# A hybrid encoder block: the gates of three token blocks as one stream of batches, the choice of experts by four ranks at a time, weights split a block ahead, and a wider output projection

## The chip, the core and the metric

The kernel runs on one core of a Trainium2 chip. The metric is the device time of one execution in microseconds (us); the time of a version is the median of its runs. The engines of the core are named as the profile names them: PE is TensorE (its matmuls), PEld its weight loads, DVE is VectorE, ACT is ScalarE, POOL is GpSimd, SP is SyncE, which issues most of the loads. Each engine works off its own queue in order, and an instruction that waits holds up what stands behind it in that queue.

## What is computed

One layer on 512 tokens of width 1024, in float32: `h = x + Mixer(RMSNorm(x))`, `h = h + PEER(RMSNorm(h))`, then a last RMSNorm. The mixer is one wide input projection, a gated recurrence (HGRN2), a long convolution by Fourier transforms (Hyena), two gated branch projections and an output projection `w_out`. PEER is a lookup of experts. For 8 heads a query is compared with two sets of 128 keys; the best 16 of each side give 256 sums, and the best 16 of these name 16 of 16384 experts:

```python
s1, i1 = lax.top_k(s[:, :, 0], PEER_TOPK)
s2, i2 = lax.top_k(s[:, :, 1], PEER_TOPK)
cand_s = (s1[..., :, None] + s2[..., None, :])          # 16 x 16 sums
top_s, pos = lax.top_k(cand_s, PEER_TOPK)
experts = jnp.take_along_axis(cand_i, pos, axis=-1)
g = jax.nn.softmax(top_s, axis=-1)
act = jax.nn.gelu(jnp.einsum('td,thkd->thk', xb, u)) * g   # u, v: rows of two tables
return jnp.einsum('thk,thkd->td', act, v)
```

## The kernel before

Tokens come in four blocks of 128. A float32 product is made of three matmuls on values split into a high part and a residual: `split` (lines 90 to 94) rounds on ACT (L93) and subtracts on DVE (L94), and `mm3` (lines 97 to 105) issues high by high and low by high in turn (L102, L103), then high by low (L105). A weight block of 1024 x 128 is loaded by SP, split into `whi` and `wlo` (two buffers each) and multiplied: 24 matmuls of 512 columns.

The mixer comes first. Its last part, `projected`, multiplies the merged branches by `w_out`. The split weights of `w_out` lie in four pairs of tiles of 256 columns (`load_wo`), so that each token block takes 4 times 24 matmuls of 256 columns (L1176), and each group of 24 is added to `h` by DVE (L1177).

`queries` then computes the scores of the 16 half heads (`hp`), each from one block of the weights `w_q`: a product (`proj`), a copy `qT` and a score product, and five DVE instructions per token block that find the best 16 (`top16`).

The experts are used in two ways. Token block 0 (`GTB`) fetches the rows of its chosen experts from memory with indirect loads by POOL. Token blocks 1, 2 and 3 (`DTB`, the dense blocks) are multiplied with all 16384 experts: a row `r` of 128 experts is 24 matmuls of 384 columns into `ps_a` (two buffers) and a gelu on ACT (`act_row`); later `combine` multiplies the gated result with the rows of the second table, 18 matmuls of 512 columns a row. For this the gates of the chosen experts have to be spread out into a matrix of 128 x 128 experts for each token.

That spreading is the part around the change:

- `select` picks, for four heads of one token block, the 16 best of 50 candidate sums and their expert numbers. It compares the positions with a list (`one`, L1288, bfloat16), multiplies with the candidate numbers (`exp`, L1290) and adds up (L1281). It works on two heads and eight ranks at a time; ranks 0 to 7 need only 20 of the 50 candidates. Four steps, two of 20 candidates (320 elements) and two of 50 (800 elements), make one call, and each token block takes two calls, one for each half of the heads (`part` 0 and 1). `one` is written with the rank innermost and read by L1290 with the candidate innermost, so that its neighbours in the reading lie 8 bfloat16 apart.
- `gates_out` takes one dense block. DVE splits each expert number into two indices `i1`, `i2` (L1313 to L1317), PE turns these and the gates (three transposes, L1323), ACT copies them out as `tr` and `tg` (L1324, L1325). Then come 32 batches of four tokens: DVE compares (`one`, L1334) and multiplies (`own`, L1337), ACT copies (`rows`, L1336), PE multiplies `own` by `rows` (L1344), four batches behind the preparation (`LAG`), and ACT copies the product to `Gs` (L1349), which SP writes to memory after eight batches. After its 32 batches a block runs its last five steps with no new batch, and then the next block's turning begins.
- `main` in `peer` strings this together: the last `select` of the first dense block, then for each block its `gates_out` with one step of the next block's `select` (for the last block: of the top 16 of token block 0) after every third step (`mixed`, `MIX`). `weave` puts one `act_row` in for each unit of a hand-set cost. `select` of token block 0 and the first steps of `combine` follow.

The order of the instructions on each engine is not the order of the code: a scheduler makes it from the dependencies, its own estimate of each duration, and the order of the code as priority. The order on each engine is then fixed.

Of the kernel before, what the change touches and what calls it, by code (L numbers as in the profile page):

```python
# [21 lines left out]
P = 128  # L22
L = 512
D = 1024
# [119 lines left out]
def proj(C, src, xh, xl, eng=None):  # L144

    hi, lo = load_w(C, src, eng=eng)
# [63 lines left out]
def mixer(C):  # L210
# [40 lines left out]

    def gates_b():
# [25 lines left out]
    with tc.tile_pool(name="yah", bufs=1, side="right") as yp:  # L278
# [11 lines left out]
        C.wos = []  # L290
# [12 lines left out]

def load_wo(C, pool, c):

    nc = C.nc
    if c % 2 == 0:
        C.wos.append((pool.tile([P, KB, 2 * P], F32R, name=f"woh{c}"), pool.tile([P, KB, 2 * P], F32R, name=f"wol{c}")))
    hi, lo = C.wos[c // 2]
    o = (c % 2) * P  # L310
# [11 lines left out]
def hyena(C, ctx, xh, xl, raws, fill):  # L322
# [112 lines left out]
    for half in range(D // HC):  # L435
# [94 lines left out]
        for fb in range(4):  # L530
# [16 lines left out]
            split(nc, Yi[0][:, fb], Yi[1][:, fb], t3)  # L547
        next(fill)
# [299 lines left out]
MIX = 3  # L848
# [3 lines left out]
LAG = 4  # L852
GQ = 32
# [16 lines left out]
def peer(C, ctx, mh, ml):  # L870
# [9 lines left out]
    pio = cp.tile([P, NPAIR, TOPK // 2], BF16, name="pio")  # L880
    with tc.tile_pool(name="pid", bufs=1) as ip:
        pid = ip.tile([P, NPAIR], F32, name="pid")
        nc.scalar.dma_start(pid, a["pair"].to_broadcast([P, NPAIR]))
        nc.vector.tensor_copy(pio, pid[:, :, None].to_broadcast([P, NPAIR, TOPK // 2]))
# [65 lines left out]
    with tc.tile_pool(name="gb", bufs=1) as gb, tc.tile_pool(name="slw", bufs=2) as sw, \  # L950
# [209 lines left out]
def projected(C, mh, ml, xh, xl, xg):  # L1160

    nc, tc, a = C.nc, C.tc, C.a
    with tc.tile_pool(name="wo4", bufs=1) as w4, tc.tile_pool(name="wo2", bufs=2) as wo2:
# [6 lines left out]
        for tb in range(TB):  # L1170
# [18 lines left out]
def queries(C, xh, xl, v16, i16, s0, chosen, fill):  # L1189
# [3 lines left out]
    with tc.tile_pool(name="slc", bufs=1) as cp, tc.tile_pool(name="slw0", bufs=2) as w2, tc.tile_pool(name="slw1", bufs=2) as sw:  # L1193
# [48 lines left out]
def select(C, w2, tb, part, v16, i16, gate, eid, pio, ahead=2):  # L1242
# [40 lines left out]
    H2, K2 = 2, TOPK // 2  # L1283
    for hd in range(0, H, H2):
        for k0, n in ((0, NFIRST), (K2, NPAIR)):
# [190 lines left out]
```

## Time and profile before

| | us |
|---|---|
| runs shown | 2046.88, 2050.67, 2050.99; median 2050.67 |
| profiled execution | 2054.18 |
| its span | 2052.4 |
| PE busy in it | 2020.1 (98%) |
| DVE busy in it | 1681.6 (82%) |
| ACT busy in it | 991.3 (48%) |
| POOL busy in it | 545.2 (27%) |

The span is the time from the first to the last instruction of the program on the core; 1.8 us of the profiled execution lie outside it. Places in the profile are given in us from the start of the span. The output projection runs from 723 to 771, `queries` to about 940, the gates of the dense blocks to 1163, and the last stage, rows and `combine` beside the fetched rows of token block 0, to the end. In rows of the timeline the columns are start, length, engine, line, operation and tiles, and in brackets the idle time of that engine just before, with what ended it. A matmul's length is longer than its distance to the next one, since matmuls overlap.

### The profile page before, as it was taken

Reading aid. Unit: us, or ns where it says so; the run is one execution under the profiler, and the core shown is the slowest. Engines: PE = TensorE matmul, PEld = TensorE weight load, DVE = VectorE, ACT = ScalarE, POOL = GpSimd, SP = SyncE. Lnnn points to the kernel's source line nnn. Section 1 sums busy time; section 2 is a strip of 40 time slices with the busy share of each in tenths; the row PEclk is TensorE's granted clock in tenths of the full one; section 3 lists DMA queues with packets and bytes.
Section 4 is the critical chain, followed back from the end, with each engine's and each line's share of the span. In section 5 each row is a group of like instructions: output and inputs, shape, how many; then the busy total and the mean of one; then the engine's idle time right before and its main releaser. Section 6 shows DMA issues by size and latency. Waiting matters only on the chain.

```text
span 2052.4 us, 30757 instructions
## 1 busy us (share of the span) xinstructions
PE 2020.1 (98%) x11625; PEld 1787.2 (87%) x11625; DVE 1681.6 (82%) x3036; ACT 991.3 (48%) x1473; POOL 545.2 (27%) x331
## 2 busy tenths in 40 slices
PE   8999999999999999999999999999999999999998
PEld 6888888888888898899999998888888888888887
DVE  6788853989986647979999877886887789889895
ACT  5555434777775623436776643333323323333333
POOL 0000000000000000000000017766766777766760
PEclk9999999999999999999999999999999999999999
DMA  5212213212122434224767788988998898999884
GB/s 193 84 52 68 72 52 112 72 63 79 66 73 73 152 127 144 98 72 159 223 189 241 234 305 335 338 317 316 347 345 302 322 367 334 350 345 343 317 295 171
DMA packets 160402, 417.96 MB, mean 204 GB/s; under 512 B 12890, under 2 KB 66012, under 8 KB 160126
## 3 DMA queue, kind: packets, MB, share of 16 engines
q1 hardware_dynamic: 115180, 263.58, 37.4%
q0 software_dynamic: 36864, 134.23, 17.8%
q10 hardware_dynamic: 8210, 18.19, 2.5%
q8 instruction: 91, 1.49, 0.3%
q14 instruction: 57, 0.47, 0.1%
HBM read 377.94 MB, written 38.01 MB: 203 GB/s over the span
## 4 chain that ended last, share of the span: by engine, by line
PE 85%; DVE 7%; DMA 3%; issue 3%; ACT 1%; POOL 0%; DVEq 0%; ACTq 0%; SPq 0%; POOLq 0%
PE ps_mm L102 10%; PE ps_mm L105 10%; PE ps_mm L103 10%; PE acc L1072 7%; PE acc L1073 7%; PE acc L1071 7%; PE ps_a L103 7%; PE ps_a L102 7%; PE ps_a L105 7%; PE ps_g L1344 3%; PE ps_x L666 1%; DMA grow<-in_u,gidx 1%; PE ps_x L102 1%; PE ps_x L105 1%; PE ps_x L103 1%
## 5 line engine op out<-in xcount | busy, mean ns | idle before, releaser
L102 PE MATMUL ps_a<-pxh,uh 128*128 128x384 f32 x1024 | 347.6, 339 | 4.6 <-ACT gact L931 4.5
L103 PE MATMUL ps_a<-pxl,uh 128*128 128x384 f32 x1024 | 345.0, 337 | 0.0
L94 POOL TENSOR_TENSOR ul<-uraw,uh 128x1024 fp32r<-128x1024 f32 x70 | 184.8, 2640 | 595.6 <-PE ps_a L105 446.2
L93 ACT CAST vh<-vraw 128x1024 fp32r<-128x1024 f32 x128 | 134.5, 1051 | 351.1 <-DMA vraw<-in_v 246.9
L1072 PE MATMUL acc<-vl,gh 128*128 128x512 f32 x768 | 300.6, 391 | 3.0 <-DVE vl L94 3.0
L1073 PE MATMUL acc<-vh,gl 128*128 128x512 f32 x768 | 300.2, 391 | 0.0
L1071 PE MATMUL acc<-vh,gh 128*128 128x512 f32 x768 | 298.8, 389 | 0.0
L102 PE MATMUL ps_mm<-xh,whi 128*128 128x512 f32 (+1 forms) x656 | 256.5, 393 | 0.4 <-ACT gt L255 0.4
L103 PE MATMUL ps_mm<-xl,whi 128*128 128x512 f32 (+1 forms) x656 | 252.2, 386 | 0.0
L1014 DVE SCALAR_TENSOR_TENSOR grow<-grow,xg 128x1024 f32<-128x1024 f32 x128 | 191.3, 1516 | 52.9 <-DMA grow<-in_u,gidx 52.8
L1026 DVE SCALAR_TENSOR_TENSOR xg<-grow,gw,xg 128x1024 f32<-128x1024 f32 x127 | 196.5, 1547 | 29.9 <-DMA grow<-in_v,gidx 28.3
L902 POOL IOTA iota<- 128x512 bf16 x1 | 1.2, 1189 | 770.8 <-PE ps_mm L105 770.8
L985 POOL DMA_INDIRECT grow<-in_u,gidx x128 | 188.7, 1474 | 51.1 <-issue 22.1
L102 PEld LDWEIGHTS ps_a<-pxh,uh 128*128 128x128 f32 x1024 | 193.2, 189 | 8.9 <-ACT gact L931 5.9
L105 PE MATMUL ps_a<-pxh,ul 128*128 128x384 f32 x1024 | 198.2, 334 | 0.0
L103 PEld LDWEIGHTS ps_a<-pxl,uh 128*128 128x128 f32 x1024 | 193.1, 189 | 3.0
L94 DVE TENSOR_TENSOR vl<-vraw,vh 128x1024 fp32r<-128x1024 f32 x128 | 180.4, 1410 | 3.4 <-ACT vh L93 3.4
L94 DVE TENSOR_TENSOR wlo<-wraw,whi 128x1024 fp32r<-128x1024 f32 x112 | 136.6, 1220 | 54.9 <-PE ps_mm L105 29.2
L985 POOL DMA_INDIRECT grow<-in_v,gidx x128 | 170.3, 1330 | 36.9 <-issue 20.2
L105 PEld LDWEIGHTS ps_a<-pxh,ul 128*128 128x128 f32 x1024 | 179.3, 188 | 0.1
L93 ACT CAST whi<-wraw 128x1024 fp32r<-128x1024 f32 x112 | 117.4, 1049 | 120.8 <-PE ps_mm L103 110.8
L93 ACT CAST uh<-uraw 128x1024 fp32r<-128x1024 f32 x128 | 134.5, 1051 | 84.9 <-PE ps_a L103 63.9
(417 smaller groups left out, 4079.7 us busy)
## 6 DMA issues: line engine op xcount, KB each, us to landing
uraw<-in_uT SPq DMA_DIRECT2D x128, 512.0 KB, 6.1
vraw<-in_v SPq DMA_DIRECT2D x128, 512.0 KB, 6.0
wraw<-in_w_in SPq DMA_DIRECT2D x80, 512.0 KB, 3.5
Gd<-Gs SPq DMA_DIRECT2D x12, 2048.0 KB, 9.7
gt<-Gd SPq DMA_DIRECT2D x32, 768.0 KB, 7.4
kept<-gact ACTq DMA_DIRECT2D x22, 384.0 KB, 3.5
gkept<-kept SPq DMA_DIRECT2D x22, 384.0 KB, 5.8
wraw<-in_w_q SPq DMA_DIRECT2D x16, 512.0 KB, 4.4
```

The lines of the kernel that those rows point to most:

```text
L93: nc.scalar.copy(hi, src)
L94: return (eng or nc.vector).tensor_sub(lo, src, hi).ins
L102: nc.tensor.matmul(out, ah, bh, start=(i == 0), stop=False)
L103: nc.tensor.matmul(out, *((al, bh) if late else (ah, bl)), start=False, stop=False)
L105: nc.tensor.matmul(out, *((ah, bl) if late else (al, bh)), start=False, stop=(stop and i == n - 1))
L985: nc.gpsimd.indirect_dma_start(out=t, out_offset=None, in_=tab, in_offset=bass.IndirectOffsetOnAxis(ap=gidx[:, j : j + 1], axis=0))
L1014: nc.vector.scalar_tensor_tensor(t, t, 1.0, xg, op0=ALU.mult, op1=ALU.mult, accum_out=gdot[h][:, i : i + 1])
L1026: nc.vector.scalar_tensor_tensor(gacc, t, gw[h][:, i : i + 1], gacc, op0=ALU.mult, op1=ALU.add)
L1071: nc.tensor.matmul(acc[k][c], gh[:, ts_], vh[:, ds_], start=(r == 0), stop=False)
L1072: nc.tensor.matmul(acc[k][c], gh[:, ts_], vl[:, ds_], start=False, stop=False)
L1073: nc.tensor.matmul(acc[k][c], gl[:, ts_], vh[:, ds_], start=False, stop=(r == NK - 1))
L1344: nc.tensor.matmul(pg[:, q * P : q * P + P], own[:, q], rows[:, q], start=True, stop=True)
```

## The change

Five edits.

1. `w_out`: the first four column blocks now share one pair of tiles of 512 columns, the others stay at 256 (`WIDE`). A token block takes 24 matmuls of 512 and 48 of 256 columns, and one addition of 512 and two of 256 columns.
2. Weights ahead: `queries` calls `load_w` (load, round, subtract) for the next block of `w_q` ahead of the product of the present one. `gates_b` does the same for the last four of its eight blocks (`C.early`).
3. `select` works on four heads and four ranks at a time (`RANKS`): again two steps of 320 and two of 800 elements a call, with the neighbours read by the multiplication now 4 bfloat16 apart.
4. `gates_out` is split. `gates_in` holds the indices, the transposes and the copies; it is issued at the end of the next block's `select`, while batches of the present block still run.
5. `gates_out` is now one stream of 96 batches over the three blocks, with no run-out between them, and `MIX` is 3, 2, 3 for the three blocks.

```diff
+def product(C, w, xh, xl):
+    hi, lo = w
...
     def gates_b():
+        w = None
         for db in range(KB):
-            ps = proj(C, a["w_in"][72 + db], xh, xl)
-            nc.scalar.activation(gts[db], ps, AF.Sigmoid)
+            now = w or load_w(C, a["w_in"][72 + db])
+            w = load_w(C, a["w_in"][73 + db]) if C.early and db < KB - 1 else None
+            nc.scalar.activation(gts[db], product(C, now, xh, xl), AF.Sigmoid)
...
+WIDE = {0: 4 * P, 4: 2 * P, 6: 2 * P}
...
-MIX = 3
+MIX = (3, 2, 3)
+RANKS = 4
...
+        ready = []
+        def chosen_and_turned(k):
+            yield from weighed(DTB[k], [part for part in range(2) if part or k >= EARLY])
+            ready.append(gates_in(C, gb, ps_g, DTB[k], gate, eid))
+            yield BATCH
         def main():
-            rest = [weighed(tb, [part for part in range(2) if part or k >= EARLY]) for k, tb in enumerate(DTB)]
-            yield from rest[0]
-            for k, tb in enumerate(DTB):
-                nxt = rest[k + 1] if k + 1 < len(DTB) else best(sw)
-                yield from mixed(gates_out(C, gb, go, ps_g, k, tb, gate, eid, iota), nxt, MIX)
+            yield from chosen_and_turned(0)
+            batches = gates_out(C, gb, go, ps_g, ready, iota)
+            for k in range(len(DTB)):
+                nxt = chosen_and_turned(k + 1) if k + 1 < len(DTB) else best(sw)
+                yield from mixed(islice(batches, P // 4), nxt, MIX[k])
+            yield from batches
...
-            for c, (hi, lo) in enumerate(C.wos):
+            for c, (hi, lo) in C.wos.items():
+                w = WIDE[c]
                 ps = C.ps_mm.tile([P, L], F32, name="ps_mm")
-                mm3(nc, ps[:, :256], [((mh[:, k, ts_], ml[:, k, ts_]), (hi[:, k], lo[:, k])) for k in range(KB)])
-                nc.vector.tensor_add(h[:, c * 256 : c * 256 + 256], ps[:, :256], h[:, c * 256 : c * 256 + 256])
+                mm3(nc, ps[:, :w], [((mh[:, k, ts_], ml[:, k, ts_]), (hi[:, k], lo[:, k])) for k in range(KB)])
+                nc.vector.tensor_add(h[:, c * P : c * P + w], ps[:, :w], h[:, c * P : c * P + w])
...
+        ahead = load_w(C, a["w_q"][2])
         for hp in range(16):
-            scores(hp, C.first[hp] if hp < 2 else proj(C, a["w_q"][hp], xh, xl))
+            if hp < 2:
+                ps = C.first[hp]
+            else:
+                wq, ahead = ahead, load_w(C, a["w_q"][hp + 1]) if hp < 15 else None
+                ps = product(C, wq, xh, xl)
+            scores(hp, ps)
...
-    H2, K2 = 2, TOPK // 2
-    for hd in range(0, H, H2):
-        for k0, n in ((0, NFIRST), (K2, NPAIR)):
-            one = w2.tile([P, H2, NPAIR, K2], BF16, name="one", bufs=2)
...
+    for k0 in range(0, TOPK, RANKS):
+        n = NFIRST if k0 + RANKS <= TOPK // 2 else NPAIR
+        one = w2.tile([P, H, NPAIR, RANKS], BF16, name="one", bufs=2)
...
-def gates_out(C, gb, go, ps_g, k, tb, gate, eid, iota):
+def gates_in(C, gb, ps_g, tb, gate, eid):
...
+    return tr, tg
+def gates_out(C, gb, go, ps_g, ready, iota):
+    nc = C.nc
     NB = P // 4
+    n = len(DTB) * NB
     made, prods = {}, {}
-    for b in range(NB + LAG + 1):
-        if b < NB:
+    for b in range(n + LAG + 1):
+        if b < n:
+            tr, tg = ready[b // NB]
+            j = b % NB
```

The scheduler turns this into other orders at the following places. Up to the output projection (edit 2 in `gates_b` included) the order on every engine is the same as before, and on ACT it is the same up to the middle of the first dense block's gates.

DVE in `queries`, beside the top 16 of one half head and a `select` of token block 1. Before (the subtraction for the next weight block stands a half head later, outside these rows):

```order
L1361 MAX_INDEX i_7639<-v_7638,s 128x8
L1362 MATCH_REPLACE rest<-v_7638,s 128x128
L1290 TENSOR_TENSOR exp<-one,ci 128x16x20
L1363 MAX v_7638<-rest 128x8
L1288 TENSOR_TENSOR one<-pio,cpf 128x800
L1364 MAX_INDEX i_7639<-v_7638,rest 128x8
L1290 TENSOR_TENSOR exp<-one,ci 128x800
```

The same place of the changed kernel:

```order
L1399 MAX_INDEX i_7533<-v_7532,s 128x8
L1400 MATCH_REPLACE rest<-v_7532,s 128x128
L94 TENSOR_TENSOR wlo<-wraw,whi 128x1024
L1401 MAX v_7532<-rest 128x8
L1317 TENSOR_TENSOR one<-pio,cpf 128x800
L1402 MAX_INDEX i_7533<-v_7532,rest 128x8
L1319 TENSOR_TENSOR exp<-one,ci 128x800
```

The subtraction `wlo` of a weight block now stands one half head earlier in DVE's queue.

PE where the second dense block's numbers are turned. Before:

```order
L105 MATMUL ps_a<-pxh,ul 128x384 x8
L1344 MATMUL ps_g<-rows,own 128x128 x20
L1323 MATMUL ps_g<-ident,i_10059 128x128
L1323 MATMUL ps_g<-ident,i_10060 128x128
L1323 MATMUL ps_g<-ident,gate 128x128
L102 MATMUL ps_a<-pxh,uh 128x384
```

The same transposes in the changed kernel:

```order
L105 MATMUL ps_a<-pxh,ul 128x384 x8
L1381 MATMUL ps_g<-rows,own 128x128 x8
L1352 MATMUL ps_g<-ident,i_9796 128x128
L1352 MATMUL ps_g<-ident,i_9797 128x128
L1352 MATMUL ps_g<-ident,gate 128x128
L1381 MATMUL ps_g<-rows,own 128x128 x16
```

Before, all 32 batches (4 matmuls each) of the first block stood ahead of the transposes and two rows without a batch followed them; now 20 batches stand ahead of them, and batches of the first block follow at once. From the first transposes to the last batch the changed order holds 30 rows of experts, the order before 31; that row now follows the last batch.

SP at the start of the last stage. Before, the loads of `vraw` (rows of the second table), `gt` (gates) and `gkept` among those of `uraw`:

```order
L910 DMA uraw<-in_uT 128x1024
L1037 DMA vraw<-in_v 128x1024
L910 DMA uraw<-in_uT 128x1024
L1037 DMA vraw<-in_v 128x1024
L1046 DMA gt<-Gd 128x1536
L910 DMA uraw<-in_uT 128x1024
L1037 DMA vraw<-in_v 128x1024
L910 DMA uraw<-in_uT 128x1024
L1037 DMA vraw<-in_v 128x1024
```

The same loads in the changed kernel:

```order
L925 DMA uraw<-in_uT 128x1024
L1060 DMA vraw<-in_v 128x1024
L925 DMA uraw<-in_uT 128x1024
L1060 DMA vraw<-in_v 128x1024
L1069 DMA gt<-Gd 128x1536
L925 DMA uraw<-in_uT 128x1024
L1060 DMA vraw<-in_v 128x1024 x2
L925 DMA uraw<-in_uT 128x1024
```

Two loads of `vraw` that had one of `uraw` between them now stand next to each other.

More of the change, by code (lines that the diff above doesn't have):

```diff
@@ L144, in proj @@
 def proj(C, src, xh, xl, eng=None):
-    hi, lo = load_w(C, src, eng=eng)
+    return product(C, load_w(C, src, eng=eng), xh, xl)
+def product(C, w, xh, xl):
+    hi, lo = w
     ps = C.ps_mm.tile([P, L], F32, name="ps_mm")
@@ L301, in mixer @@
     return mh, ml
+WIDE = {0: 4 * P, 4: 2 * P, 6: 2 * P}
 def load_wo(C, pool, c):
     nc = C.nc
[L307 to L310, printed above, removed]
+    first = max(f for f in WIDE if f <= c)
+    if c == first:
+        C.wos[c] = [pool.tile([P, KB, WIDE[c]], F32R, name=f"wo{x}{c}") for x in "hl"]
+    hi, lo = C.wos[first]
+    o = (c - first) * P
     raw = C.wraw.tile([P, KB, P], F32, name="wraw")
@@ L547, in hyena @@
             split(nc, Yi[0][:, fb], Yi[1][:, fb], t3)
+        C.early = half == D // HC - 1
         next(fill)
@@ L879, in peer @@
     i16 = {GTB: cp.tile([P, 16, TOPK], U32, name="i16g")}
-    pio = cp.tile([P, NPAIR, TOPK // 2], BF16, name="pio")
+    pio = cp.tile([P, NPAIR, RANKS], BF16, name="pio")
     with tc.tile_pool(name="pid", bufs=1) as ip:
@@ L883, in peer @@
         nc.scalar.dma_start(pid, a["pair"].to_broadcast([P, NPAIR]))
-        nc.vector.tensor_copy(pio, pid[:, :, None].to_broadcast([P, NPAIR, TOPK // 2]))
+        nc.vector.tensor_copy(pio, pid[:, :, None].to_broadcast([P, NPAIR, RANKS]))
     gidx = cp.tile([P, P], I32, name="gidx")
@@ L1281, in reduce @@
         nc.vector.reduce_sum(out, terms, axis=AX.X)
-    H2, K2 = 2, TOPK // 2
-    for hd in range(0, H, H2):
-        for k0, n in ((0, NFIRST), (K2, NPAIR)):
-            one = w2.tile([P, H2, NPAIR, K2], BF16, name="one", bufs=2)
-            terms = w2.tile([P, H2, K2, NPAIR], F32, name="exp", bufs=ahead + 1)
-            nc.vector.tensor_tensor(one[:, :, :n], pio[:, None, :n].to_broadcast([P, H2, n, K2]),
-                                    cpf[:, hd : hd + H2, None, k0 : k0 + K2].to_broadcast([P, H2, n, K2]), op=ALU.is_equal)
-            nc.vector.tensor_mul(terms[:, :, :, :n], one[:, :, :n].rearrange("p h j k -> p h k j"),
-                                 ci[:, hd : hd + H2, None, :n].to_broadcast([P, H2, K2, n]))
-            out = eid[:, tb, ks].rearrange("p (h k) -> p h k", k=TOPK)[:, hd : hd + H2, k0 : k0 + K2]
-            found.append((out, terms[:, :, :, :n]))
-            if len(found) > ahead:
-                reduce()
-            yield 0.7 if k0 == 0 else 1.3
-        if hd == 0:
+    for k0 in range(0, TOPK, RANKS):
+        n = NFIRST if k0 + RANKS <= TOPK // 2 else NPAIR
+        one = w2.tile([P, H, NPAIR, RANKS], BF16, name="one", bufs=2)
+        terms = w2.tile([P, H, RANKS, NPAIR], F32, name="exp", bufs=ahead + 1)
+        nc.vector.tensor_tensor(one[:, :, :n], pio[:, None, :n].to_broadcast([P, H, n, RANKS]),
+                                cpf[:, :, None, k0 : k0 + RANKS].to_broadcast([P, H, n, RANKS]), op=ALU.is_equal)
+        nc.vector.tensor_mul(terms[:, :, :, :n], one[:, :, :n].rearrange("p h j k -> p h k j"),
+                             ci[:, :, None, :n].to_broadcast([P, H, RANKS, n]))
+        out = eid[:, tb, ks].rearrange("p (h k) -> p h k", k=TOPK)[:, :, k0 : k0 + RANKS]
+        found.append((out, terms[:, :, :, :n]))
+        if len(found) > ahead:
+            reduce()
+        yield 0.7 if n == NFIRST else 1.4
+        if k0 == RANKS:
             nc.scalar.activation(ex, ex, AF.Exp)
```

12 lines of the change are left out of this document (7 added, 5 removed).

## The prediction

> **What bounds the kernel now.** I read the page's busy times first, then the chain of work that ended last, then busy times by stretch, and then, engine by engine, the places where PE stood still.
>
> ```profile
> PE 2020.1 (98%) x11625; PEld 1787.2 (87%) x11625; DVE 1681.6 (82%) x3036; ACT 991.3 (48%) x1473; POOL 545.2 (27%) x331
> PE 85%; DVE 7%; DMA 3%; issue 3%; ACT 1%; POOL 0%; DVEq 0%; ACTq 0%; SPq 0%; POOLq 0%
> ```
>
> PE is busy for 98% of the span, and 85% of the chain that ended last is PE work. So a change can gain in two ways only: by less work on PE, or by taking away the few microseconds in which PE stands still. These are the stretches around the change; the columns are start and end, length, then busy time (and number of instructions) of PE, PEld, DVE, ACT and POOL, the granted clock, and the load of the DMA engines.
>
> ```profile
> 723.00:771.00 48.00, 48.00 (x403) 47.95 (x402) 18.37 (x29) 10.14 (x20) 0.00 (x0) 1.00 0.38 132
> 917.00:942.00 25.00, 23.21 (x135) 22.92 (x134) 25.00 (x117) 11.98 (x15) 0.00 (x0) 1.00 0.38 120
> 942.00:1101.00 159.00, 154.87 (x1073) 153.78 (x1072) 158.97 (x443) 111.85 (x189) 0.00 (x0) 1.00 0.65 197
> 1101.00:1163.00 62.00, 61.70 (x446) 61.73 (x447) 54.39 (x133) 46.66 (x79) 0.00 (x0) 1.00 0.79 242
> 1163.00:1200.00 37.00, 34.15 (x198) 33.51 (x196) 36.79 (x92) 21.03 (x29) 0.00 (x0) 1.00 0.85 279
> 1200.00:1260.00 60.00, 60.00 (x308) 56.33 (x309) 41.37 (x47) 21.02 (x26) 30.35 (x18) 0.97 0.89 327
> 1260.00:2052.00 792.00, 782.30 (x3798) 690.85 (x3796) 661.59 (x617) 273.57 (x338) 513.42 (x308) 1.00 0.87 321
> ```
>
> From 917 to 1101 DVE has no free moment (25.00 of 25.00, 158.97 of 159.00) while PE loses 1.79 and 4.13. There DVE sets the pace and PE waits for it now and then; elsewhere PE sets it. From 1260 on nothing is changed.
>
> **The wider product.** PE alone bounds 723 to 771. The starts of the third part of successive groups of 24 matmuls, from the chain, first at 256 columns, then at 512:
>
> ```profile
> 749.14 0.96 PE ps_mm L105 x8
> 752.02 0.96 PE ps_mm L105 x8
> ...
> 292.64 1.81 PE ps_mm L105 x8
> 298.08 1.81 PE ps_mm L105 x8
> ```
>
> A group of 256 columns takes 752.02 - 749.14 = 2.88, one of 512 takes 5.44. Two narrow ones become a wide one: 2 x 2.88 - 5.44 = 0.32 less for each of four token blocks, **-1.28**. DVE, busy for 18.37 of 48, covers the wider addition; the last group of each token block is as narrow as before, so what follows it is as late as before. All six blocks of split weights that the loops of the mixer load are ready long before, and the last of the merged branches is needed only by the fifteenth matmul. The term depends on a fixed cost of some 13 ns a matmul (5.44/24 = 227 and 2.88/24 = 120 ns). [...] The rows here say 13 ns, and I take them.
>
> **Weights a block ahead.** In `gates_b` the order on all engines stays the same, so nothing. In `queries` it takes one wait:
>
> ```profile
> 845.78 1.06 ACT L93 CAST whi<-wraw 128x1024 fp32r<-128x1024 f32 x1 [2.20 <-PE ps_mm L103]
> ...
> 856.61 1.21 DVE L94 TENSOR_TENSOR wlo<-wraw,whi 128x1024 fp32r<-128x1024 f32 x1
> ...
> 857.88 0.50 PE L105 MATMUL ps_mm<-pxh,wlo 128*128 128x512 f32 x1 [1.31 <-DVE wlo L94]
> ```
>
> ACT has rounded the block at 846.8; DVE subtracts only ten microseconds later, behind a `select` and a top 16, and PE waits 1.31. In the changed order the subtraction stands a half head earlier: **-1.3** (between 0 and that). The price: DVE may now wait for ACT's rounding, which PE releases; behind it stand searches of the top 16, for which nobody waits until 917. SP's queue here changes only in that loads of `uraw` and `wraw` alternate.
>
> **Four ranks.** The rows of `exp`, whose reading of `one` steps 16 bytes from neighbour to neighbour, in two sizes; of `own`, which reads in the same way in steps of 8 bytes; of a plain subtraction of 1024; and of the two compares, one in groups of four (L1334) and one in groups of eight (L1288):
>
> ```profile
> L1290 DVE TENSOR_TENSOR exp<-one,ci 128x800 f32<-128x800 bf16 x16 | 25.7, 1607 | 0.0
> L1290 DVE TENSOR_TENSOR exp<-one,ci 128x320 f32<-128x320 bf16 x16 | 11.7, 734 | 0.0
> L1337 DVE TENSOR_TENSOR own<-one,tg 128x512 f32<-128x512 bf16 x96 | 63.3, 687 | 0.7 <-PE ps_g L1344 0.6
> L94 DVE TENSOR_TENSOR ul<-uraw,uh 128x1024 fp32r<-128x1024 f32 x58 | 70.4, 1216 | 8.0 <-ACT uh L93 8.0
> L1334 DVE TENSOR_TENSOR one<-iota,tr 128x1024 bf16<-128x1024 bf16 x96 | 62.3, 688 | 0.0
> L1288 DVE TENSOR_TENSOR one<-pio,cpf 128x800 bf16<-128x800 bf16 x16 | 9.1, 571 | 0.0
> ```
>
> `exp` costs (1607 - 734)/480 = 1.82 ns an element. `own` takes 687 for 512 and the plain subtraction 1216 for 1024, on one line at (1216 - 687)/512 = 1.03 an element; so a step of 8 bytes costs nothing extra. With its neighbours 8 bytes apart I put `exp` on that line: 687 + 288 x 1.03 = 985 for 800, 687 - 192 x 1.03 = 489 for 320. A call of `select` has two of each: 2 x (622 + 245) = **1.73 less on DVE**. The compare does not suffer: in groups of four it takes 688 for 1024, on the line of 571 for 800. If the distance is not the cause, the saving is zero. It is PE time only where PE waits for DVE: one call lies in 917 to 942, three between 942 and 1101, two after it.
>
> **The first turning.**
>
> ```profile
> 916.35 0.49 DVE L1360 MAX8 v<-s 128x8 f32<-128x128 f32 x2 [5.60 <-ACT s L1205]
> ...
> 941.54 0.22 DVE L1317 TENSOR_SCALAR i<-i 128x128 f32<-128x128 f32 x1
> ...
> 941.86 0.41 PE L1323 MATMUL ps_g<-ident,i 128*128 128x128 f32 x2 [1.78 <-issue]
> ```
>
> DVE starts at 916.35, when the last scores come, and runs without a pause until the indices are done at 941.7. PE has been waiting 1.78. The order of both engines stays, so 1.73 less on DVE is 1.7 less waiting; I take **-1.6** (0 to -1.78).
>
> **From block to block.** These are the waits inside the gates, and the one on ACT behind the second.
>
> ```profile
> 1000.28 1.13 PE L1344 MATMUL ps_g<-rows,own 128*128 128x128 f32 x8 [1.34 <-DVE i L1317]
> ...
> 1011.33 0.26 ACT L1298 ACTIVATE ex<-ex 128x64 f32<-128x64 f32 x1 [2.25 <-DVE ex L1273]
> ...
> 1022.45 0.45 PE L102 MATMUL ps_a<-pxh,uh 128*128 128x384 f32 x1 [1.65 <-ACT gact L931]
> ...
> 1101.30 0.68 PE L1344 MATMUL ps_g<-rows,own 128*128 128x128 f32 x4 [1.37 <-ACT rows L1336]
> ```
>
> They lie where one block ends and the next begins: a batch behind the indices on DVE, a gelu that ACT reaches late behind an exponential and the new block's copies, and the new block's first `rows`. Together 4.36. In the changed order batches of the old block stand behind the transposes, and three calls take 5.2 off DVE, more than the waits. But the second block's transposes come earlier on PE, after 20 batches and 8 rows. At 0.89 a batch and 4.16 a row,
>
> ```profile
> 1026.89 2.68 PE ps_g L1344 x24
> ...
> 1204.54 1.39 PE ps_a L105 x8
> 1208.70 1.39 PE ps_a L105 x8
> ```
>
> (2.68 for three batches of eight records; 1208.70 - 1204.54) PE is there 20 x 0.89 + 8 x 4.16 = 51 after the first ones. DVE went from the first block's indices at 941.7 to the second's, just ahead of 1000.28, in 58.5; its new order holds three `own`, two `one` and a `ul` fewer on that way (5 x 0.69 + 1.2 = 4.7) and a faster call, 58.5 - 4.7 - 1.7 = 52.1. So PE may wait there for some 1.1; with a little for the third block's, I leave 1.5 of the 4.36: **-2.9** (0 to -4.36). I add **+0.5** for new waits where the order is new. Moving one row behind the last batch leaves PE's work the same.
>
> **The tail.**
>
> ```profile
> 1180.44 0.26 ACT L1298 ACTIVATE ex<-ex 128x64 f32<-128x64 f32 x1 [2.65 <-DVE ex L1273]
> ...
> 1184.95 0.44 PE L102 MATMUL ps_a<-pxh,uh 128*128 128x384 f32 x1 [0.66 <-ACT gact L931]
> ...
> 1198.43 1.04 ACT L93 CAST vh<-vraw 128x1024 fp32r<-128x1024 f32 x1 [4.12 <-DMA vraw<-in_v]
> ...
> 1199.92 0.45 PE L102 MATMUL ps_a<-pxh,uh 128*128 128x384 f32 x1 [2.20 <-ACT gact L931]
> ...
> 1200.48 0.53 PE L102 MATMUL ps_a<-pxh,uh 128*128 128x384 f32 x1
> 1200.81 0.53 PE L103 MATMUL ps_a<-pxl,uh 128*128 128x384 f32 x1
> ```
>
> At 1184.95 the gelu stands behind an exponential for which DVE was late; two faster calls take that away: **-0.6** (0 to -0.66). At 1199.92 it stands behind a `vh` that waits for a load; the DMA engines are at 0.85 to 0.89 there, the loads are the same and as dense, so I leave this wait, **0**. After it matmuls lie 0.33 apart (1200.48 to 1200.81) where 0.17 is usual: the clock drops for some 3.4 us, 1.7 lost. If the wait goes, both go: 2.20 + 1.7 = 3.9. [...] The trace has the drop right behind the wait.
>
> **The sum.** -1.28 - 1.3 - 1.6 - 2.9 + 0.5 - 0.6 = **-7.2**. The profiled execution took 2054.18 with its span of 2052.4; it would be 2047.0. It lies 3.5 above the median of the runs, 2050.67; the waits are taken to be the same in these, and the prediction is 2050.67 - 7.2 = **2043.5**. 0.2% (4.1 us) is about what a measurement of this kernel can tell from no change: faster is under 2046.6, slower over 2054.8.
>
> **Rivals.** *The tail's wait goes too* (17%): the gates end some 6 us earlier on PE, and if SP's loads then start earlier by as much, `vraw` lands in time. Against it: the loads stand as close, two `vraw` even next to each other. 2043.5 - 3.9 = 2039.6.
>
> *The waits form again elsewhere* (17%): only the product and the weights gain, 2050.67 - 2.6 = 2048.1. For it: the last block now holds 38 batches behind its transposes instead of 32, all top-16 searches of block 0 among them, and DVE has only 62 - 54.39 = 7.6 free in that stretch now; six more batches are 6 x 2 x 0.69 = 8.3 of DVE. Against it: DVE enters the stretch ahead of PE, by up to the buffers' six batches.
>
> *Four ranks are no faster* (7%): `exp` stays at 1607; the first turning keeps its wait, half of the block-to-block waits and of the tail's go by the new order alone: -1.28 - 1.3 - 1.75 + 0.5 = -3.8, 2046.9.
>
> *Slower* (6%): the start of the last stage. Five `vh` stand in ACT's queue ahead of gelus there, and one waits long now. If the earlier end of the gates pushes SP's loads together while the DMA engines are at 0.89, each of the five may wait as that one does: four more at 3.9 are +15.6, and 2043.5 + 15.6 = 2059.1. It decides from three more on (11.7 against 7.2 and the 4.1 that can be told).
>
> The forecast itself has 53%, with 2041.3 (all terms whole, no new waits) to 2047 as its own range. The range takes in the rival at 2039.6 with its terms whole (2.2 less, 2037) and the one at 2048.1 with the two microseconds by which the runs differ: 2037 to 2050.5. Faster: most of the forecast, the first rival, parts of the second and third: 0.67; the same: 0.27; slower: 0.06.
>
> **What would show it.** In the changed profile: groups of 512 columns in the output projection and h's last addition 1.3 earlier; no wait of PE for `wlo` in `queries`; `exp` at about 0.98 and 0.49 us; the first transposes' wait at 0.2 or less; the waits of PE between them and the last batch at about 2 in all; DVE with free time in that stretch. The prediction is wrong if `exp` is as slow as now, if PE's waits in the gates sum to over 3.5, or if PE waits for gelus behind `vh` more than once.

## The result and the profile after

The changed kernel takes **2035.56 us** (median of 4 runs, 2034.93 to 2035.66); the kernel before took 2049.28 beside it (4 runs, 2046.88 to 2050.99). The ratio is 0.9929, 95% interval 0.9916 to 0.9942: 13.7 us less where 7.2 were forecast, below the lower end of the range, 2037. Five more runs of the changed kernel gave 2035.27 (2034.77 to 2036.06).

The page's busy times and its chain of waits, of the changed kernel:

```profile
PE 2015.0 (99%) x11529; PEld 1782.1 (88%) x11529; DVE 1671.5 (82%) x3032; ACT 993.2 (49%) x1473; POOL 548.7 (27%) x331
PE 94%; DVE 4%; issue 1%; ACT 1%; DMA 1%; ACTq 0%; DVEq 0%; SPq 0%
```

DVE's share of the chain has gone from 7 to 4%, PE's from 85 to 94. The stretches of the gates at the same times as before (this kernel is some 4 us ahead there), and then the tail, counted as before from the first row behind the last batch, which starts at 1150 here and at 1163 in the kernel before:

```profile
723.00:771.00 48.00, 48.00 (x319) 44.17 (x317) 18.44 (x26) 10.53 (x21) 1.19 (x1) 1.00 0.39 135
917.00:942.00 25.00, 24.93 (x146) 24.64 (x145) 25.00 (x124) 11.62 (x17) 0.00 (x0) 1.00 0.44 153
942.00:1101.00 159.00, 158.40 (x1111) 158.24 (x1110) 158.73 (x432) 117.41 (x199) 0.00 (x0) 1.00 0.64 198
1150.00:1187.00 37.00, 36.71 (x214) 36.39 (x213) 36.83 (x96) 24.42 (x32) 0.00 (x0) 1.00 0.90 306
1187.00:1247.00 60.00, 60.00 (x318) 56.32 (x317) 41.95 (x46) 22.14 (x27) 31.29 (x19) 1.00 0.90 330
```

From 917 to 1101 DVE is as full as it was (25.00 and 158.73), but PE now loses 0.07 and 0.6 where it lost 1.79 and 4.13: both engines are full at once. In the tail, too, DVE is as full as it was (36.83 of 37 us, 36.79 before), while PE loses 0.29 where it lost 2.85; behind it the clock is 1.00, where it was 0.97. DVE has not become free in the gates or in the tail. All waits of PE from 770 to the end, in us in total, times and the longest, of the changed kernel and then of the kernel before:

```profile
PE ps_g L1352 <- DVE i16f L1279: 0.6, 1, 0.6
PE ps_a L102 <- ACT gact L946: 0.3, 1, 0.3
PE ps_mm L102 <- ACT pxh L208: 0.2, 1, 0.2
PE ps_mm L103 <- DVE pxl L209: 0.2, 1, 0.2
```

```profile
PE ps_a L102 <- ACT gact L931: 4.5, 3, 2.2
PE acc L1072 <- DVE vl L94: 3.0, 3, 1.7
PE ps_g L1323 <- issue: 1.8, 1, 1.8
...
PE ps_s L1202 <- ACT qT L1199: 0.7, 1, 0.7
```

Nothing of note is left. To see where the time went, take the starts on PE of the same piece of work in both profiles: the first product with `w_q` on the last tokens (below: the first product of `queries`), the first transposes (941.86 before), the first row behind the last batch, and the first `acc`. Of the kernel before and of the changed one:

```profile
778.86 0.50 PE L102 MATMUL ps_mm<-pxh,whi 128*128 128x256 f32 x2 [0.24 <-ACT pxh L203]
...
1163.23 0.42 PE L102 MATMUL ps_a<-pxh,uh 128*128 128x384 f32 x1
...
1226.56 0.39 PE L1071 MATMUL acc<-vh,gh 128*128 128x512 f32 x1
```

```profile
777.38 0.50 PE L102 MATMUL ps_mm<-pxh,whi 128*128 128x256 f32 x2 [0.24 <-ACT pxh L208]
...
937.57 0.41 PE L1352 MATMUL ps_g<-ident,i 128*128 128x128 f32 x2
...
1150.23 0.42 PE L102 MATMUL ps_a<-pxh,uh 128*128 128x384 f32 x1
...
1213.32 0.39 PE L1094 MATMUL acc<-vh,gh 128*128 128x512 f32 x1
```

One row of 4.16 has moved from the gates to the tail. So, in us of these two profiles:

| stretch | forecast | measured |
|---|---|---|
| up to the first product of `queries` | -1.28 | 777.38 - 778.86 = -1.5 |
| `queries`, to the first transposes | -1.3 - 1.6 = -2.9 | -4.3 + 1.5 = -2.8 |
| gates, to the row behind the last batch | -2.9 + 0.5 = -2.4 | -13.0 + 4.3 + 4.16 = -4.5 |
| tail, to the first `acc` | -0.6 | -13.2 + 13.0 - 4.16 = -4.4 |
| last stage, to the end | 0 | -18.5 + 13.2 = -5.3 |
| sum | -7.2 | -18.5 |

18.5 is the difference of the spans, 2052.4 and 2033.9. The profiled execution of the kernel before took 2054.18, 4.9 above the median beside which 13.7 was measured; the experiments come back to that. The first three rows are close to the forecast or better; the last two, but for 0.6, were not in it. The 5.3 of the last stage is time in which PE waited for `vl`. The matmuls wait 3.0 for it in the kernel before, but the weight loads, which come ahead of them, wait 5.0; in the changed kernel neither wait:

```profile
PEld acc L1072 <- DVE vl L94: 5.0, 5, 2.1
```

It is lost in one stretch: the two profiles are still 13.4 apart at the `acc` that starts at 1528.4 before and at 1514.9 in the changed kernel, and 18.3 at that of 1632.4 and 1614.1.

### The profile page after: what moved, and what is told of

Same layout as the page of the kernel before. It is cut to its first block, busy times and chain, and to the rows that moved or that the text cites. A ratio compares the mean times of both kernels' runs of the same rounds, so it can differ in the third digit from the quotient of the medians.

```text
span 2033.9 us, 30551 instructions
## 1 busy us (share of the span) xinstructions
PE 2015.0 (99%) x11529; PEld 1782.1 (88%) x11529; DVE 1671.5 (82%) x3032; ACT 993.2 (49%) x1473; POOL 548.7 (27%) x331
## 4 chain that ended last, share of the span: by engine, by line
PE 94%; DVE 4%; issue 1%; ACT 1%; DMA 1%; ACTq 0%; DVEq 0%; SPq 0%
PE ps_mm L102 11%; PE ps_mm L105 10%; PE ps_mm L103 10%; PE acc L1095 9%; PE acc L1094 9%; PE acc L1096 9%; PE ps_a L103 8%; PE ps_a L102 8%; PE ps_a L105 8%; PE ps_g L1381 3%; PE ps_x L680 1%; PE ps_x L102 1%; PE ps_x L105 1%; PE ps_x L103 1%; PE ps_s L1226 1%
## 5 line engine op out<-in xcount | busy, mean ns | idle before, releaser
L1049 DVE SCALAR_TENSOR_TENSOR xg<-grow,gw,xg 128x1024 f32<-128x1024 f32 x127 | 191.3, 1506 | 29.9 <-DMA grow<-in_v,gidx 28.4
L94 DVE TENSOR_TENSOR vl<-vraw,vh 128x1024 fp32r<-128x1024 f32 x128 | 193.8, 1514 | 3.6 <-ACT vh L93 3.6
```

The costliest lines, as they stand in the source:

```text
L94: return (eng or nc.vector).tensor_sub(lo, src, hi).ins
L1049: nc.vector.scalar_tensor_tensor(gacc, t, gw[h][:, i : i + 1], gacc, op0=ALU.mult, op1=ALU.add)
```

## The experiments

### A second profile of the kernel before (`b_again`)

> The kernel before, unchanged, for a second profile of it. If the waits of PE belong to the program, the same ones come again within 0.3 us each: 1.3 for wlo, 1.8 at the first transposes, 1.3, 1.65 and 1.4 between the blocks, 0.7 and 2.2 at the tail with the slow clock behind it, and 3.0 for vl between 1528 and 1580; the time is then near 2054. If the waits for vl in the last stage belong to one execution (its gathers come when they come), they are of another size here, and the time is 2047 to 2051, with the waits before 1215 as they were.

Measured: 2052.44. The same waits came again, all within 0.3 us up to 1200. In the last stage the waits for `vl` are 2.3 us in place of 3.0, one of them at the same place and of the same size. The profile before, then this one, lines of PE's timeline:

```profile
1568.30 0.50 PE L1072 MATMUL acc<-vl,gh 128*128 128x512 f32 x1 [1.68 <-DVE vl L94]
...
1578.07 0.50 PE L1072 MATMUL acc<-vl,gh 128*128 128x512 f32 x1 [1.20 <-DVE vl L94]
```

```profile
1566.29 0.50 PE L1072 MATMUL acc<-vl,gh 128*128 128x512 f32 x1 [0.47 <-DVE vl L94]
...
1576.06 0.50 PE L1072 MATMUL acc<-vl,gh 128*128 128x512 f32 x1 [1.20 <-DVE vl L94]
```

So the waits up to 1200 belong to the program; those for `vl` came twice, in different sizes. The slow clock belongs to the execution: the long wait of the tail is there again, 2.16 at 1200.26, but the stretch behind it ran at full speed. The column ahead of the last two is the granted clock; this run, then the kernel before:

```profile
1200.00:1204.00 4.00, 3.74 (x21) 3.74 (x22) 3.02 (x7) 2.52 (x4) 0.00 (x0) 1.00 0.94 365
```

```profile
1200.00:1204.00 4.00, 4.00 (x14) 4.00 (x15) 3.55 (x8) 2.84 (x4) 0.00 (x0) 0.57 0.86 291
```

### Four ranks alone (`b_ranks`), the stream alone (`b_stream`), four ranks for token block 0 alone (`b_ranks_tail`)

The kernel before with edit 3 alone; with edits 4 and 5 alone; and with the choice of eight ranks for the dense blocks and of four for block 0:

```diff
-        return select(C, pool, tb, part, v16, i16, gate, eid, pio, ahead)
+        pick, pos = (select, pio) if tb == GTB else (select8, pio8)
+        return pick(C, pool, tb, part, v16, i16, gate, eid, pos, ahead)
```

> The kernel before with four ranks at a time in select, nothing else. Theory A (DVE's time in select is what all those waits hang on): exp takes 0.98 and 0.48 us, the first transposes wait 0.2 or less, the three waits between the blocks fall by half or more, and the tail's waits of 0.7 and 2.2 go with the slow clock behind: 1.7 + 2 + 0.6 + 3.9 = 8 us less. Theory B (the new order of the gates removes them, four ranks only the first one): 2 us less, with the waits between the blocks and at the tail still there.

> The kernel before with the gates as one stream and the early transposes, the old select. Theory A: exp stays at 1.6 and 0.73 us, DVE is as late as before; the first transposes wait 1.8, the waits between the blocks only move: 0 to 2 us less. Theory B: the waits between the blocks (4.4) and the tail's (0.7, and 3.9 with the clock) go: 7 to 9 us less.

> The kernel before with four ranks only in the select of token block 0, the last two calls; the order of PE and POOL is the same, that of ACT and SP but for a few instructions. Theory C (the vh of the tail is late because SP's load of vraw stands behind a load of uraw whose buffer DVE frees late): the calls are 1.7 us shorter, vraw is issued 1 to 2 us earlier, the tail's waits of 0.7 and 2.2 go and the clock stays at full speed: 4 to 5 us less. Theory D (the load itself is slow beside the others): only the wait of 0.7 goes, 0.7 us less or no change that can be told.

Measured, with the kernel before at 2051.17 beside them: four ranks alone 2045.43, ratio 0.9976 [0.9967, 0.9985], 4.9 us less by the ratio (5.7 by the medians); the stream alone 2048.93, 0.9991 [0.9981, 1.0001], no change that can be told; four ranks for block 0 alone 2047.21, 0.9988 [0.9977, 0.9998], 2.5 us less by the ratio (4.0 by the medians).

Neither theory A nor B holds: each part removes waits and makes a new one. Four ranks alone leave no wait at the first transposes, none for `wlo`, none in the tail; but at the second block's first batch PE, ACT and DVE read:

```profile
1011.06 0.38 PE L1338 MATMUL ps_g<-ident,i 128*128 128x128 f32 x2
...
1020.35 3.63 PE L1359 MATMUL ps_g<-rows,own 128*128 128x128 f32 x16 [4.29 <-ACT rows L1351]
```

```profile
1018.43 1.85 ACT L1351 CAST rows<-one 128x512 f32<-128x512 bf16 x3 [4.60 <-DVE one L1349]
```

```profile
1016.63 1.05 DVE L1276 TENSOR_TENSOR ci<-i1x,i16f 128x32 f32<-128x32 f32 x11
1017.59 0.21 DVE L1375 MAX8 ctop<-cs 128x8 f32<-128x50 f32 x1
1017.72 1.88 DVE L1349 TENSOR_TENSOR one<-iota,tr 128x1024 bf16<-128x1024 bf16 x3
```

PE has turned the numbers at 1011, but DVE makes the first `one` at 1017.7, behind steps of the next choice (`cs`, `ci`, `ctop`); nothing of the old block is left to run meanwhile, and the clock drops behind the wait (0.57 from 1020 to 1024). The stream alone keeps the slow multiplications, and DVE is late for everything:

```profile
PE ps_g L1376 <- DVE own L1369: 3.3, 3, 1.9
PE ps_g L1347 <- DVE i L1341: 2.1, 1, 2.1
PE ps_g L1347 <- issue: 1.8, 1, 1.8
```

Theory C holds for half of what it explains. In the kernel before, DVE and then SP read in the tail:

```profile
1189.88 1.21 DVE L94 TENSOR_TENSOR ul<-uraw,uh 128x1024 fp32r<-128x1024 f32 x1
```

```profile
1191.12 0.33 SPq L910 DMA_DIRECT2D uraw<-in_uT  x1
1191.50 0.43 SPq L1037 DMA_DIRECT2D vraw<-in_v  x1
```

The load of `vraw` on which the gelu waited stands on SP behind a load of `uraw`, and that one waits until DVE has subtracted the last `ul` from its buffer: the subtraction ends at 1191.09, and SP issues at 1191.12. DVE had run behind since the choice for block 0 began (busy for 20.00 of 20.00 us from 1180 to 1200). With four ranks for that choice alone, SP and ACT read:

```profile
1189.29 0.33 SPq L927 DMA_DIRECT2D uraw<-in_uT  x1
1189.67 0.91 SPq L1054 DMA_DIRECT2D vraw<-in_v  x2
```

```profile
1194.83 1.05 ACT L93 CAST vh<-vraw 128x1024 fp32r<-128x1024 f32 x1 [0.99 <-DMA vraw<-in_v]
```

The load starts 1.8 us earlier, `vh` 3.6 us earlier (1194.83 against 1198.43), and neither the wait of 2.2 nor the slow clock is there (1.00 from 1200 to 1204). The wait of 0.7 stays. The other 1.8 of the 3.6 is the load itself: from its issue to the end of ACT's wait it took 6.9 us before (1198.43 - 1191.50) and 5.2 here (1194.83 - 1189.67). In the second profile of the kernel before it took 7.1 (1198.77 - 1191.64), and the wait of 2.16 was there. Two kernels that come below leave the tail as it was, `b_ahead` and `b_lightdot`. There SP issues as late, at 1191.38 and 1192.10, but the load takes 5.0 and 4.5; PE does not wait at this place, only 0.3 and 0.8 a row later; the clock is 1.00 in `b_ahead` from 1163 to 1200 and in `b_lightdot` from 1160 to 1220. SP and ACT of `b_ahead`:

```profile
1191.38 0.43 SPq L1052 DMA_DIRECT2D vraw<-in_v  x1
```

```profile
1196.39 1.05 ACT L93 CAST vh<-vraw 128x1024 fp32r<-128x1024 f32 x1 [2.38 <-DMA vraw<-in_v]
```

So the late issue alone does not make the wait of 2.2. In the four profiles with the old tail it came only where the load was slow as well, as theory D had it. What makes the load slow in some executions is not shown. The time fell by 0.4 to 4.7 us by the interval, where 4 to 5 were expected: 2.2 and 1.7 were the price in one execution, not in every one.

### The step alone (`a_step8`), and the old choice for block 0 (`a_slowtail`)

The changed kernel with `one` padded; and with eight ranks for token block 0:

```diff
-        one = w2.tile([P, H, NPAIR, RANKS], BF16, name="one", bufs=2)
+        one = w2.tile([P, H, NPAIR, 2 * RANKS], BF16, name="one", bufs=2)[:, :, :, :RANKS]
```

> The changed kernel with one change: the tile one of select is padded to eight ranks, of which four are used, so that the multiplication reads again in steps of 16 bytes, with the instructions, their number and PE's order as in the changed kernel. If the step is the cause, exp takes 1.6 and 0.73 us again, DVE has 13 us more in eight calls, and the waits of PE come back in part: 5 to 10 us more than the changed kernel's 2035.6, so 2041 to 2046. If the new grouping (four heads, four ranks) is the cause and not the step, exp stays at 0.98 and 0.48 and the time at 2035 to 2037.

> The changed kernel with the old select (eight ranks) for token block 0 alone, its last two calls; the order of PE, ACT, SP and POOL is that of the changed kernel. If the four ranks of these calls keep the tail free, the wait of some 2 us at the vh comes back, with the slow clock: 3 to 4.5 us more than 2035.6. If the tail is free because DVE enters it earlier, there is slack: in the changed kernel the late vh at 1181.09 made no wait, and 1.7 us more make 0 to 1 us.

Measured, beside 2048.93 of the kernel before: 2043.91, ratio 0.9974 [0.9964, 0.9984], and 2037.03, 0.9940 [0.9927, 0.9954]. The groups of `exp` of the changed kernel, then of the padded one, where the last figures are busy us and mean ns:

```profile
L1319 DVE TENSOR_TENSOR exp<-one,ci 128x800 f32<-128x800 bf16 x16 | 15.6, 978 | 0.0
...
L1319 DVE TENSOR_TENSOR exp<-one,ci 128x320 f32<-128x320 bf16 x16 | 7.3, 481 | 0.0
```

```profile
L1319 DVE TENSOR_TENSOR exp<-one,ci 128x800 f32<-128x800 bf16 x16 | 25.8, 1614 | 0.0
L1319 DVE TENSOR_TENSOR exp<-one,ci 128x320 f32<-128x320 bf16 x16 | 11.2, 729 | 0.0
```

The step between neighbours is the whole cause of the faster `exp`: same instructions, same sizes, 16 bytes in place of 8. It is worth some 8 us to the changed kernel (2043.91 against 2035.56, medians of two series), and the waits that come back are like those of the stream alone: 1.8 and 2.4 at the transposes, 1.5 for `own`, 1.4 in the tail. Why the wider step is slower was not shown.

With the old choice for block 0 the late `vh` did not come back; the one wait that grew (2.0, from 0.3) is that of a gelu behind the exponential of this choice. So this execution of the changed kernel did without the faster choice in the tail. SP and ACT of the changed kernel at the same load of `vraw`:

```profile
1175.88 0.43 SPq L1060 DMA_DIRECT2D vraw<-in_v  x1
```

```profile
1181.09 1.05 ACT L93 CAST vh<-vraw 128x1024 fp32r<-128x1024 f32 x1 [1.19 <-DMA vraw<-in_v]
```

Counted from the first row behind the last batch, SP issues it 25.7 us in (1175.88 - 1150.23), and 28.3 in the kernel before (1191.50 - 1163.23). These 2.6 us are more than the wait of 2.2. But here, too, the load was short: 5.2 us, and 4.5 with the old choice (1180.51 - 1176.04). Whether a slow load would make PE wait in the changed kernel was not seen.

### Block by block (`a_nostream`, `a_nostream_mix`), turning late (`a_lateturn`), the other mix (`a_mix3`)

The changed kernel without edits 4 and 5; without them but with the mix 3, 2, 3; as a stream whose numbers are turned when a block's first batch is made; and as a stream with the mix 3, 3, 3:

```diff
-            ready.append(gates_in(C, gb, ps_g, DTB[k], gate, eid))
+            ready.append(k)
...
-            tr, tg = ready[b // NB]
             j = b % NB
+            if j == 0:
+                tr, tg = gates_in(C, gb, ps_g, DTB[ready[b // NB]], gate, eid)
```

> The changed kernel with the gates block by block as before (four ranks, the wide product and the weights ahead stay). If the parts add up, it has the 4.45 us wait for rows that four ranks alone showed in the old order (DVE in the third block's select ahead of the second block's batches), and the time is 2045.4 less 1.3 for the product and 2.3 for the weights: 2041 to 2042.5, 6 us over the changed kernel. If the weights ahead had taken that wait too, 2036 to 2038.

> The changed kernel with the gates block by block as before, but with the mix 3, 2, 3. If the run-out between the blocks makes the wait of 4.5 us at the second block's first rows, it is there again: 2042, like block by block with the mix 3. If the mix made it, 2036 to 2038.

> The changed kernel as one stream of batches, but with the indices and transposes of a block only when its first batch is made, behind all batches of the block before. If the early turning is what removes the long wait for rows (4.5 us in the old order with four ranks), a wait of 2 to 4.5 us is back at the start of the second or third dense block: 2038 to 2041. If it is the stream without a run-out and the other mix, 2035 to 2037.

> The changed kernel with three batches to a step of select in all three blocks (3, 3, 3) in place of 3, 2, 3. With 3 the third block's choice is spread over 42 batches where 32 are there, so a rest of it comes in a heap at the end of the second block. If the stream without a run-out is what hides the waits, 2035 to 2037; if the mix is, a wait of PE of 2 us or more stands near the third block's first batches (about 1085 to 1100): 2038 to 2041.

Measured: block by block 2042.48, ratio 0.9965 [0.9951, 0.9978]; with the mix 3, 2, 3 2040.31, 0.9952 [0.9940, 0.9965]; turned late 2035.64, 0.9940 [0.9926, 0.9953]; mix 3, 3, 3 2036.00, 0.9930 [0.9917, 0.9943]. Block by block, the long wait is there with either mix, at the second block's start or at the third's; the first of these lines is of the mix 3, the second of 3, 2, 3:

```profile
1018.44 3.76 PE L1365 MATMUL ps_g<-rows,own 128*128 128x128 f32 x16 [4.44 <-ACT rows L1357]
```

```profile
1089.82 1.22 PE L1365 MATMUL ps_g<-rows,own 128*128 128x128 f32 x8 [2.74 <-DVE own L1358]
```

In the stream it is not there, with either mix, and with the numbers turned early or late. So of edits 4 and 5 the part that counts is the missing run-out: while DVE makes a new block's first batches, PE still has the last batches of the old one. That is worth 5 to 7 us with the fast `exp`, and nothing that can be told with the slow one. The early turning and the mix brought nothing that can be told.

### The weights ahead (`a_noahead`, `b_ahead`) and the wider product (`a_nowide`)

> The changed kernel without the weights ahead. By the profiles two waits of PE come back in queries, 1.5 us for wlo and 0.9 for qT: 2.4 us more than 2035.6, 2038. If the scores' later end is caught up in the gates, where DVE sets the pace only in part: less than 1 us.

> The kernel before with the weights ahead alone. If the waits in queries are DVE's lateness behind the old select, this takes them: 1.5 for wlo and 0.9 for qT, 2.4 us less than the kernel before. If the weights ahead do nothing for them, the waits are still at 786 and 856, and the time is that of the kernel before. With the changed kernel they brought nothing, since there the faster select had taken the wait for wlo already.

> The changed kernel with four products of 256 columns. [...]

Each is one edit taken out of the changed kernel or put alone into the kernel before. Measured: without the weights ahead 2035.25, ratio 0.9937 [0.9923, 0.9950]; the weights ahead alone 2049.16 beside 2049.39, 0.9997 [0.9988, 1.0006]; without the wider product 2038.42, 0.9948 [0.9935, 0.9960]. The weights ahead brought nothing that can be told either way. Where they stand alone the wait for `wlo` goes, as forecast, but 0.55 comes back at a copy of `qT` 13 us later, and the interval does not exclude the 1.3 of the forecast. In the changed kernel the fast `exp` is enough against the wait for `wlo`: without the weights ahead `queries` has no wait but the two of 0.2 at its very start.

Without the wider product 2.9 us come back, where the 13 ns a matmul from the prediction's rows give 1.3. One part more is seen, a wait of 0.8 for the first `qT`, which none of the kernels with the wider product has over 0.2. These two make 2.1; the rest is less than the runs of this kernel differ by (2037.49 to 2040.89).

### An eighth less dot product (`b_lightdot`, `a_lightdot`), the changed kernel again (`a_again`)

```diff
-            nc.vector.scalar_tensor_tensor(t, t, 1.0, xg, op0=ALU.mult, ...
+            nc.vector.scalar_tensor_tensor(t[:, :DOT], t[:, :DOT], 1.0, xg[:, :DOT], op0=ALU.mult, ...
```

> The kernel before; it leaves out an eighth of the dot products of the first table's fetched rows of token block 0 (896 of 1024 columns), so DVE has about 0.13 us less for each of 128 rows, 17 us in the first half of the last stage. Theory E (DVE's lead over PE there runs out near 1570, and these waits for vl, 3 to 5 us in two profiles, are part of the time of the kernel before and of its spread): the waits for vl go, the median falls by 2 to 4 us and the spread of its runs shrinks. Theory F (those waits are chance of single executions and rare): the median is the same within 1 us.

> The changed kernel with the same eighth of the dot products left out. Theory E: its lead did not run out (1.7 us at the least by the profile), so nothing is won: 2035 to 2036. If the last stage of the changed kernel had waits too in most runs, 1 us or more less.

> The changed kernel once more, for the spread of its runs and a second profile. Theory E: no waits for vl, runs within 2 us of each other near 2035.6. Otherwise a spread like that of the kernel before, 5 us or more.

Measured, beside 2049.77 of the kernel before: 2047.16 (2045.18 to 2048.63), ratio 0.9990 [0.9981, 0.9999]; 2035.63 (2034.63 to 2036.11), 0.9934 [0.9920, 0.9947]; 2035.27, 0.9933 [0.9920, 0.9947]. The dot products took 29 us less of DVE in the kernel before (162.0 in place of 191.3, by the rows of their groups), more than the 17 expected. No wait for `vl` is left there, and the median falls by 2.6 (0.2 to 3.9 by the interval); the changed kernel gains nothing. So theory E fits: the waits for `vl` were some 2 to 3 us of the median, and the changed kernel has none. They are not in every execution: the profiles of `b_stream`, `b_ranks_tail` and `b_ahead`, whose code in the last stage is the old one, show none, and that of `b_ranks` 0.6. Not all of the spread is theirs: 3.4 us of it stayed.

Why DVE's lead lasts in the changed kernel is less sure. It enters the last stage earlier: its first dot product on a fetched row starts 7.2 us behind PE's first `acc` (1220.5 and 1213.3), against 8.8 before (1235.4 and 1226.6). But the stream alone entered at 8.7 (1234.3 and 1225.6) and had no wait for `vl` either. Whether the way the fetched rows arrive plays a part was not shown.

### The place of the tiles (`a_pad416`, `a_pad800`)

`queries` lost waits of 4.3 us (1.5 for `wlo`, 1.7 at the transposes, 0.8 for the first `qT`, the rest small; by the starts on PE in the kernel before and in the version with 800 bytes below) but became only 2.8 shorter. The matmuls with w_q's blocks lie 232 ns apart in the changed kernel and 228 before; in `b_ranks`, too, they lie 233 apart ((804.83 - 803.43)/6). With four ranks alone `pio` takes 400 bytes of a partition and not 800, so that the tiles behind it lie elsewhere.

```diff
-    pio = cp.tile([P, NPAIR, RANKS], BF16, name="pio")
+    pio = cp.tile([P, 2 * NPAIR, RANKS], BF16, name="pio")[:, :NPAIR]
```

> The changed kernel with the tile pio grown from 400 to 416 bytes a partition (16 unused), the order on every engine unchanged. If the tiles behind it lie badly because 400 is no multiple of 32, the matmuls of w_q are back at 228 ns, 336 of them by 4 ns: 1.4 us less than 2035.4, 2034. If it is another matter of place (a shift by 400 bytes), or the four ranks themselves, 232 ns and 2035 to 2036.

> The changed kernel with pio grown to the 800 bytes that it has in the kernel before, order unchanged. If the place of the tiles is the cause of the slower matmuls, by whatever rule, 228 ns and 2034. If the four ranks themselves are (their reading beside the matmuls), 232 ns and 2035 to 2036.

Measured: 2034.92, ratio 0.9928 [0.9914, 0.9941], and 2034.65, 0.9927 [0.9914, 0.9941]. Eight matmuls in a row of one product, of the changed kernel and with 800 bytes, start and length:

```profile
802.40 2.03 PE L105 MATMUL ps_mm<-pxh,wlo 128*128 128x512 f32 x8
```

```profile
801.86 1.98 PE L105 MATMUL ps_mm<-pxh,wlo 128*128 128x512 f32 x8
```

With 800 bytes the distance is 228 again and `queries` 1.4 shorter (935.80 - 777.05 = 158.75 against 937.57 - 777.38 = 160.19, from its first product to the first transposes); with 416 it stays at 232. So the place is the cause, not the ranks, and a multiple of 32 bytes isn't the rule; what the rule is stays open. The median of the version with 800 bytes is 0.6 to 0.9 us below those of the changed kernel and 0.3 below that with 416 bytes, less than can be told here from no change.

## Why the prediction was wrong

The direction, the bound and most mechanisms were right: PE sets the time, and the change gains by taking away its waits. The size was half of what came. Step by step:

- **The wider product** (-1.28): measured -1.5 to the first product of `queries`, by the rows' 13 ns a matmul. Right, and 0.8 of `qT` came with it.
- **Weights ahead** (-1.3): the wait for `wlo` went, but the faster `exp` takes it without this edit, which by itself brought nothing that can be told, with either choice. The prediction had not seen that two of its terms act on this one wait.
- **Four ranks** (985 and 489 ns, 1.73 less a call): 978 and 481 ns, and the step proved to be the cause.
- **The first turning** (-1.6): the wait of 1.78 became none, 937.57 shows no idle time. Four ranks alone do it. Right.
- **From block to block** (-2.9, +0.5 for new waits): measured -4.5. The second and third transposes, for which the prediction feared, wait 0.6 and 0.0. The new waits that I added are real only where one half of the change stands alone; together there are none, since the missing run-out covers DVE's choice and the fast `exp` keeps DVE in time. The early turning, in which I saw the danger, neither costs nor brings anything.
- **The tail** ("the loads are the same and as dense, so I leave this wait, 0"): this step failed. -4.4 in place of -0.6: 2.2 for the wait and 1.7 for the clock came on top. The loads are as dense as I said (0.90 of the DMA engines in the changed kernel, 0.85 before), and `vh` is in time all the same. I took its lateness for a fixed thing, and it had two parts that can move. SP issues the load 2.6 us earlier against PE, because it stands behind a load of `uraw` for which DVE has to free a buffer, and DVE comes there earlier. And the load took 5.2 us in place of 6.9; the cause of that stays open. I had the price (2.20 and 1.7) and the rival with 17%, but asked whether the gates end earlier, not what SP waits for, and took one execution for all: with the old tail the wait of 2.2 was in two of four profiles, and the clock behind it (1200 to 1204) was 0.57 in one of the two and 1.00 in the other.
- **The last stage** ("From 1260 on nothing is changed"): this step failed too. The code there is the same, but in the kernel before DVE's lead over PE ran out near 1570, and whether it does depends on more than the code of this stage. 5.3 us in these profiles, 2.6 by the experiment on the median. Why the lead lasts in the changed kernel stays open.
- **A sign that did not come**: DVE with free time in the gates. It is as full as before (158.73 of 159 us); PE's waits went although DVE has no time to spare.
- **The place of tiles** was no step at all: +1.4 in `queries`, by a tile that became smaller.

The profiled execution of the kernel before was one with the slow clock and the longest waits for `vl`, which is most of the way from 13.7 us by the medians to 18.5 by the profiles. To the 7.2 of the forecast come 2.1 in the gates, 2.1 in the tail without the clock (4.4 - 0.6 - 1.7) and 2.6 in the last stage: 14.0, beside 13.7 by the medians. That these meet so closely is partly luck, since the 2.1 of the tail was read in one execution and is not in every one. In `queries` the waits for `qT` and some small ones made up for the place.

## What to carry to other kernels

Where an engine that is not the bound is full for a stretch, ask of each transfer in and just behind it which instruction of that engine frees its buffer, its neighbours' in the issuing queue included. Tell a late issue from a slow load, and read both in more than one execution before a wait is priced. Where two changes act on one wait, price them together: here the faster choice alone gave 4.9 us by the ratio, the stream alone none that can be told, and both with the rest 13.7. And a stretch whose code is unchanged can still hold waits, and they can differ from execution to execution; look for the place where the lead of the engine that feeds is smallest.

## What the runs showed of the hardware

- The granted clock fell behind some of PE's waits and not behind others. Behind the wait of 2.20 in the kernel before it is 0.50 for 3.4 us (1200.24 to 1203.64), and 1.00 before and after; behind the one of 2.16 in the second profile it is 1.00 (1200 to 1208). Behind the wait of 4.29 in `b_ranks` it is 0.51 from 1020.4 to 1023.8 and 1.00 from 1024 to 1028; at the one of 4.44 in `a_nostream` 0.52 from 1017 to 1021 and 0.63 from 1021 to 1025; behind the one of 2.74 in `a_nostream_mix` 0.59 from 1090 to 1094. At the wait of 1.78 in `b_stream` it is 1.00 from 917 to 1101. What decides whether the clock falls was not shown.
- A tile that shrinks by 400 bytes a partition made matmuls on other tiles 4 ns slower, 232 against 228 (the changed kernel and `a_pad800`).
- DVE's multiplication costs 1.84 ns an element with a bfloat16 operand in steps of 16 bytes ((1614 - 729)/480, `a_step8`) and 1.04 in steps of 8 ((978 - 481)/480, the changed kernel).
